# Three Winograd quads instead of two in the gate/up blocks of a macaron layer, with silu in one ScalarE pass and the carry moved to GpSimd DMAs

## The chip, the core and the metric

The kernel runs on one core of a Trainium2 chip. The metric is the device time of one execution in microseconds, the median of several runs. The core has five engines with an instruction stream each: TensorE (PE in the profile; its weight loads are PEld), VectorE (DVE), ScalarE (ACT), GpSimd (POOL) and SyncE (SP). Data comes from HBM into SBUF by DMA; TensorE accumulates into PSUM banks. SP issues the weight loads; GpSimd issues some other DMAs.

## The reference

One layer on 256 tokens of width 2048, in float32: a feed-forward network (FFN 1), a mixer with an RWKV-7 branch and a pooling branch, and a second feed-forward network (FFN 2). Each part is normed before and after and added to the residual. Only the feed-forward networks are touched by the change:

```python
def _swiglu(x, w_gate, w_up, w_down):
    return (jax.nn.silu(x @ w_gate) * (x @ w_up)) @ w_down
...
f = _swiglu(_rmsnorm(h, ln_ffn1_pre[l]), ffn1_gate[l], ffn1_up[l], ffn1_down[l])
h = h + MACARON_WEIGHT * _rmsnorm(f, ln_ffn1_post[l])
```

Gate and up are 2048 x 5632, down is 5632 x 2048. All of it is in float32.

## The kernel before

**Products in three matmuls.** Each float32 operand is split into a high part (rounded to the matmul's float32r format) and a low part (the rest). ScalarE makes the high part of a weight tile (`wH`, a cast), VectorE the low part (`wL`, a subtraction). `mm3` (lines 171 to 175) forms one product as high x high, high x low and low x high: three matmuls of 128 x 128 by 128 x 512.

**Blocks of gate and up.** `ffn` (line 611) runs over 11 blocks of 512 hidden columns. A block multiplies 16 row groups (k) of 128 with the gate columns and then with the up columns, for two halves of 128 tokens: 16 x 2 x 2 = 64 products. Blocks 0 and 1 do all 64 (`gemm_tok`, `gemm_at`). Blocks 2 to 10 (`FAST`, line 49) go through `seven` (line 315).

**Quads.** `seven` takes two weight row groups, the first two quads' worth from the front of k, and treats them as a 2 x 2 by 2 x 2 block product (rows k and k+1, the two token halves, and the two column groups, here gate and up). In Winograd's form this needs seven products instead of eight, at the price of sums: of the activations (`sums`, line 252, made once per FFN in block 1 and kept) and of the weights, in each block. `quad` (line 351) loads two weight tiles `a` and `b` by four DMAs, forms `t13` and `t24` on VectorE (lines 367, 372, 373), and splits `a`, `b`, `t13` and `t24` into high and low parts (lines 379, 380). Its products go to four extra PSUM banks (`p1`, `p5`, `p6`, `p7`) and to the four ordinary ones (`f0`, `f1`, `l0`, `l1`). The remaining rows go in pairs (`pair`, line 342): one load of two row groups, one cast, one subtraction, four products. `spots` says after which pair of gate (part 0) and of up (part 1) a quad stands. After the last quad `merge` (line 396) copies one bank and adds the others on VectorE (line 404), calls `ev_first` for the gate's half, and at the block's end `finish` (line 412) adds the up half and calls `ev_last`.

**Evictions.** In the fast blocks `ev_f` (line 635) lets ScalarE write a sigmoid into a free PSUM bank and VectorE multiply (line 638); `ev_l` (line 641) multiplies gate and up and turns the result by VectorE's 32 x 32 block transposes (`turn`, line 566) into the tile `T1`. In blocks 0 and 1 `ev_g` and `ev_gm` do sigmoid and multiplication, and `ev_um` the rest.

**The carry.** The block transposes leave the 32 x 32 blocks in the wrong places. `carry_at` (line 584) moves them in the next block, by 16 ScalarE copies of 32 partitions x 256 (line 594) into the tile `x32`, then makes the high part (one cast, line 598) and the low part (one subtraction, line 602) of the next four row groups of `hT`, the input of down.

**Down.** `post` (line 719) runs down over four groups of 512 columns, two at a time, each pair through `seven` with 44 row groups: 6 quads in the first pair of columns and 8 in the second (`NQ`, `QUADS`, lines 47 and 48). Their activation sums are made at the start of down.

**Order of the work.** The streams of TensorE, ScalarE and VectorE are written out by a planner: `put` appends a piece of TensorE work with its duration (`MM` = 0.2265 us a matmul) to a clock, `at` puts another piece of work at a planned time, and `run` (line 110) emits all in order of these times. Each engine then runs its stream strictly in that order. `slot` (line 104) gives a split the planned time at which the buffer used `WS_BUFS` = 5 splits earlier is free:

```python
    def slot(s, end):
        s.uses.append(end)
        n = len(s.uses) - 1 - WS_BUFS
        return s.uses[n] if n >= 0 else n - 1.0
```

SP's and GpSimd's streams are ordered by the scheduler. Raw weights land in `W32_BUFS` = 4 buffers of 512 KB; all other large tiles share 33 units of 512 KB (`NUNITS`).

Of the kernel before, what the change touches and what calls it, by code (L numbers as in the profile page):

```python
# [46 lines left out]
NQ = {False: 6, True: 8}  # L47
QUADS = {False: ((8, 12), (0, 3, 6, 9)), True: ((2, 4, 6, 8, 10, 12), (1, 3))}
FAST = range(2, 11)

# [5 lines left out]
class Block:  # L56
# [195 lines left out]
    def sums(s, T, out, when, own=None):  # L252
# [6 lines left out]
        def first():  # L259
            xH, xL = T[len(out) // 2]  # L260
            x = tt["x"] = s.unit((P, 2, 2, S), F32, "sx")
            V.tensor_tensor(out=fl(x), in0=xH.bitcast(F32).rearrange("p k t -> p (k t)"),
                            in1=xL.bitcast(F32).rearrange("p k t -> p (k t)"), op=ALU.add)

        def second():
            x = tt["x"]
            a11, a21 = x[:, :, 0, :P], x[:, :, 0, P:]
            a12, a22 = x[:, :, 1, :P], x[:, :, 1, P:]
            f = tt["f"] = s.unit((P, 4, 2, P), F32, "sf")
            V.scalar_tensor_tensor(out=f[:, 0], in0=a21, scalar=-1.0, in1=a22, op0=ALU.mult,  # L270
                                   op1=ALU.subtract)
            V.scalar_tensor_tensor(out=f[:, 1], in0=f[:, 0], scalar=-1.0, in1=a11,
                                   op0=ALU.mult, op1=ALU.subtract)
            V.tensor_tensor(out=f[:, 2], in0=a11, in1=a21, op=ALU.subtract)
            V.tensor_tensor(out=f[:, 3], in0=a12, in1=f[:, 1], op=ALU.subtract)
# [26 lines left out]
        def third():  # L302
            tt["H"], tt["L"] = [s.unit((P, 4, 2, P), F32R, n_) for n_ in ("sH", "sL")]
            nc.scalar.copy(fl(tt["H"]), fl(tt["f"]))

        def fourth():
            f, fH, fL = tt["f"], tt["H"], tt["L"]
            V.tensor_tensor(out=fl(fL), in0=fl(f), in1=fl(fH).bitcast(F32), op=ALU.subtract)
            for i in range(2):
                out.append([(fH[:, m, i], fL[:, m, i]) for m in range(4)])  # L310
# [4 lines left out]
    def seven(s, wf, cf, wl, cl, at, KT, T, sm, n, spots, ev_first, ev_last, trail=False):  # L315
# [35 lines left out]
        def quad(q):  # L351
# [18 lines left out]
            def t24():  # L370
                o = v["t24"]
                V.tensor_tensor(out=o[:, 0], in0=v["a"][:, 0], in1=v["t13"][:, 1], op=ALU.add)
                V.tensor_tensor(out=o[:, 1], in0=v["b"][:, 0], in1=o[:, 0], op=ALU.subtract)
# [8 lines left out]
            for t, fn in ((a, get), (a, t13), (a, t24), (a, lambda: split("a", 2)),  # L382
                          (b, lambda: split("b", 1)), (c, lambda: split("t13", 2)),
                          (d, lambda: split("t24", 2))):
                s.at(t, fn)
# [10 lines left out]
        def merge():  # L396
# [9 lines left out]
            for j, a in enumerate(((1, "p6", 0), (2, "p7", 1), (3, "p5", 2), (1, "p5", 1),  # L406
                                   (1, "f0", 1), (3, "f1", 3))):
                s.at(m + 0.7 + 0.1 * j, lambda a=a: add(*a))
            s.at(m + 4, lambda: ev_first(0, u[1], bank["p1"]))
            s.at(m + 4.6, lambda: ev_first(1, u[3], bank["p6"]))  # L410

        def finish(h):
            o = u[2 * h]
            V.tensor_tensor(out=o, in0=bank[f"l{h}"], in1=o, op=ALU.add)
            ev_last(h, o)
# [10 lines left out]
        if trail:  # L426
            s.by_half(wl, cl, stop, KT, s.clk, AHEAD[0],
                      lambda k, h: mul(f"l{h}", rows(k, h), ws[k]), keep, finish)
            return
# [136 lines left out]
    def turn(s, T1, h, src):  # L566

        s.nc.vector.transpose(out=T1[:, h * 512:h * 512 + 512], in_=src)  # L568

    def shuffle_split(s, T1, T, j):  # L570

        nc = s.nc
        x32 = s.unit((P, 4, S), F32, "x32")
        src = T1.rearrange("p (h k j c) -> p h k j c", h=2, k=4, j=4)
        dst = x32.rearrange("p k (h i c) -> p h k i c", h=2, i=4)
        for i in range(4):
            for q in range(4):
                nc.scalar.copy(dst[q * 32:q * 32 + 32, :, :, i],
                               src[i * 32:i * 32 + 32, :, :, q])
        dH, dL = T[j]  # L580
        nc.scalar.copy(dH, x32)
        nc.vector.tensor_tensor(out=dL, in0=x32, in1=dH.bitcast(F32), op=ALU.subtract)

    def carry_at(s, T1, T, t):
# [4 lines left out]
        def one(i, q):  # L589
            src = T1[0].rearrange("p (h k j c) -> p h k j c", h=2, k=4, j=4)  # L590
            if not x:
                x.append(s.unit((P, 4, S), F32, "x32"))
            dst = x[0].rearrange("p k (h i c) -> p h k i c", h=2, i=4)
            nc.scalar.copy(dst[q * 32:q * 32 + 32, :, :, i], src[i * 32:i * 32 + 32, :, :, q])  # L594

        def high():
            T.extend(s.new_T(1))
            nc.scalar.copy(T[-1][0], x[0])

        def low():  # L600
            dH, dL = T[-1]
            nc.vector.tensor_tensor(out=dL, in0=x[0], in1=dH.bitcast(F32), op=ALU.subtract)
        for n in range(16):
            s.at(t + 0.9 * n, lambda n=n: one(n // 4, n % 4))
        s.at(t + 15, high)
        s.at(t + 17, low)
# [4 lines left out]
    def ffn(s, wg, wu, wd, uT, rs, gpost, resid, emit, reload, xs=None):  # L611
# [7 lines left out]
        def block(b):  # L619
# [8 lines left out]
            def ev_g(h, ps):  # L628
                sg = s.tmp("sg")
                nc.scalar.activation(out=sg, in_=ps, func=AF.Sigmoid, scale=rs[h])  # L630
                nc.vector.scalar_tensor_tensor(out=sg, in0=ps, scalar=rs[h], in1=sg,
                                               op0=ALU.mult, op1=ALU.mult)
                sig[h] = sg

            def ev_f(h, u, free):
                nc.scalar.activation(out=free, in_=u, func=AF.Sigmoid)
                sig[h] = u
                s.at(s.now + 1.2, lambda: nc.vector.tensor_tensor(
                    out=u, in0=u, in1=free, op=ALU.mult))

            def ev_l(h, o):
                nc.vector.tensor_tensor(out=o, in0=o, in1=sig[h], op=ALU.mult)
                turned(h, o)

            def ev_gm(h, ps):
                sg = s.tmp("sg")
                nc.scalar.activation(out=sg, in_=ps, func=AF.Sigmoid, scale=r[h])
                sig[h] = sg
                s.at(s.now + 1.2, lambda: nc.vector.scalar_tensor_tensor(
                    out=sg, in0=ps, scalar=r[h], in1=sg, op0=ALU.mult, op1=ALU.mult))  # L650
# [18 lines left out]
            if b == 1:  # L669
                st["nT"], st["su"] = s.normed(uT, st["rb"], s.clk + 4), []  # L670
                s.sums(st["nT"], st["su"], s.clk + 16)
            nT, su = st["nT"], st["su"]
            if b in FAST:
                s.seven(wg, b * 512, wu, b * 512, s.T_at(nT), NKD, nT, su, 2, ((4,), (1,)),
                        ev_f, ev_l)
                return
            x = at if b == 1 else s.T_at(nT)
            s.gemm_at(wg, b * 512, x, NKD, ev_gm)
# [40 lines left out]
    def post(s, wd, at, KT, gpost, fac, resid, emit, reload, hT=None, sm=None):  # L719
# [52 lines left out]
        if hT is not None:  # L772
# [3 lines left out]
            for c in (0, 2):  # L776
                ev = ev_of(c)
                s.seven(wd, c * 512, wd, c * 512 + 512, at, KT, hT, sm, NQ[c == 2], QUADS[c == 2],
                        lambda h, u, _, ev=ev: ev(h, u), ev_of(c + 1), c == 2)
# [761 lines left out]
```

## Time and profile before

| | |
|---|---|
| time, median of 3 runs (lowest, highest) | 2059.87 us (2057.18, 2060.95) |
| the profiled execution's own time | 2060.43 us |
| its span, first to last instruction | 2058.7 us |
| granted TensorE clock, mean | 0.999 |
| TensorE / VectorE / ScalarE / GpSimd busy | 2043.5 / 1687.5 / 1247.4 / 76.0 us |
| DMA traffic | 407.03 MB, mean 198 GB/s |

The profile is of one execution. A group row gives the line, engine, operation, output and inputs with their shapes and the count, then busy time and mean duration of one, then the idle time of the engine just before them and what ended it. A timeline row gives start, duration, engine, line and operation, with "xN" where N in a row are merged. A window row gives, for a stretch of the span, the busy time and instruction count of each engine, the granted clock, the DMA engines' share and their rate.

### The profile page before, as it was taken

Reading aid. Unit: us, or ns where it says so; the run is one execution under the profiler, and the core shown is the slowest. Engines: PE = TensorE matmul, PEld = TensorE weight load, DVE = VectorE, ACT = ScalarE, POOL = GpSimd, SP = SyncE. Lnnn points to the kernel's source line nnn. Section 1 sums busy time; section 2 is a strip of 40 time slices with the busy share of each in tenths; the row PEclk is TensorE's granted clock in tenths of the full one; section 3 lists DMA queues with packets and bytes.
Section 4 is the critical chain, followed back from the end, with each engine's and each line's share of the span. In section 5 each row is a group of like instructions: output and inputs, shape, how many; then the busy total and the mean of one; then the engine's idle time right before and its main releaser. Section 6 shows DMA issues by size and latency. Waiting matters only on the chain.

```text
span 2058.7 us, 29579 instructions
## 1 busy us (share of the span) xinstructions
PE 2043.5 (99%) x10901; PEld 1721.7 (84%) x10901; DVE 1687.5 (82%) x2188; ACT 1247.4 (61%) x1788; POOL 76.0 (4%) x161
## 2 busy tenths in 40 slices
PE   9999999999999999999999999999999999999998
PEld 7888888888888899999888888888888888888886
DVE  6898889888988865799688667578988898889886
ACT  7667666776555574474465444466677666765553
POOL 0000000000000000000110110010000000000000
PEclk9999999999999999999999999999999999999999
DMA  7566666665667766656456565665666666656674
GB/s 259 175 195 211 194 206 194 196 212 176 210 208 251 228 189 187 180 159 196 133 155 193 161 245 189 205 211 169 203 199 200 214 195 194 197 186 215 210 254 155
DMA packets 226170, 407.03 MB, mean 198 GB/s; under 512 B 15199, under 2 KB 51177, under 8 KB 226025
## 3 DMA queue, kind: packets, MB, share of 16 engines
q1 hardware_dynamic: 219849, 384.69, 59.7%
q0 software_dynamic: 5888, 19.93, 2.7%
q8 instruction: 85, 1.39, 0.3%
q10 hardware_dynamic: 288, 0.52, 0.1%
q14 instruction: 60, 0.49, 0.1%
HBM read 396.69 MB, written 8.39 MB: 197 GB/s over the span
## 4 chain that ended last, share of the span: by engine, by line
PE 92%; DVE 3%; issue 2%; DMA 2%; ACT 1%; POOL 0%; POOLq 0%; DVEq 0%; SPq 0%; ACTq 0%
PE mm L173 24%; PE mm L175 23%; PE mm L174 23%; PE mc L523 10%; PE ms L175 3%; PE ms L173 3%; PE ms L174 3%; DMA w<-in_ffn_down_dram 1%; DVE wL L150 1%; PE tr L551 1%; ACT x L594 0%; PE pA L1262 0%; ACT wH L149 0%; DVE u L404 0%; ACT wH L379 0%
## 5 line engine op out<-in xcount | busy, mean ns | idle before, releaser
L150 DVE TENSOR_TENSOR wL<-w,wH 128x1024 fp32r<-128x1024 f32 (+2 forms) x597 | 711.4, 1206 | 232.9 <-ACT wH L149 229.9
L149 ACT CAST wH<-w 128x1024 fp32r<-128x1024 f32 (+2 forms) x597 | 614.8, 1043 | 392.4 <-PE mm L175 200.5
L173 PE MATMUL mm<-wH,xH 128*128 128x512 f32 x2076 | 811.6, 392 | 0.0
L175 PE MATMUL mm<-wH,xL 128*128 128x512 f32 x2076 | 808.5, 389 | 0.7 <-DVE xL L559 0.5
L174 PE MATMUL mm<-wL,xH 128*128 128x512 f32 x2076 | 808.4, 389 | 0.7 <-DVE wL L150 0.7
L175 PEld LDWEIGHTS mm<-wH,xL 128*128 128x128 f32 x2076 | 389.7, 188 | 82.8 <-DVE xL L559 1.5
L174 PEld LDWEIGHTS mm<-wL,xH 128*128 128x128 f32 x2076 | 389.8, 188 | 81.2 <-DVE wL L150 1.6
L173 PEld LDWEIGHTS mm<-wH,xH 128*128 128x128 f32 x2076 | 389.6, 188 | 81.0 <-ACT xH L557 0.2
L379 ACT CAST wH<-t 128x1024 fp32r<-128x1024 f32 x128 | 134.5, 1052 | 72.7 <-DVE t L367 42.6
L380 DVE TENSOR_TENSOR wL<-t,wH 128x1024 fp32r<-128x1024 f32 x128 | 152.5, 1218 | 25.0 <-ACT wH L379 25.0
L379 ACT CAST wH<-w 128x1024 fp32r<-128x1024 f32 (+1 forms) x128 | 107.2, 838 | 96.7 <-PE mm L175 51.6
L523 PE MATMUL mc<-xH,wH 128*128 128x256 f32 x560 | 159.5, 285 | 0.0
L523 PE MATMUL mc<-xL,wH 128*128 128x256 f32 x560 | 158.4, 283 | 0.0
L523 PE MATMUL mc<-xH,wL 128*128 128x256 f32 x560 | 158.4, 283 | 0.0
L594 ACT COPY x<-T 32x256 f32<-32x256 f32 x352 | 142.2, 404 | 10.9 <-DVE T L568 4.6
L380 DVE TENSOR_TENSOR wL<-w,wH 128x1024 fp32r<-128x1024 f32 (+1 forms) x128 | 116.7, 950 | 1.3 <-ACT wH L379 1.3
L523 PEld LDWEIGHTS mc<-xH,wH 128*128 128x128 f32 x560 | 106.0, 189 | 1.1
L523 PEld LDWEIGHTS mc<-xH,wL 128*128 128x128 f32 x560 | 106.0, 189 | 0.2
L523 PEld LDWEIGHTS mc<-xL,wH 128*128 128x128 f32 x560 | 106.0, 189 | 0.1
L367 DVE TENSOR_TENSOR t<-w,w 128x1024 f32<-128x1024 f32 x64 | 78.0, 1218 | 16.4 <-DMA w<-in_ffn_down_dram 12.0
L174 PE MATMUL ms<-wL,sH 128*128 128x512 f32 x164 | 63.8, 389 | 0.0
L175 PE MATMUL ms<-wH,sL 128*128 128x512 f32 x164 | 63.8, 389 | 0.0
(298 smaller groups left out, 1974.7 us busy)
## 6 DMA issues: line engine op xcount, KB each, us to landing
w<-in_ffn_up_dram SPq DMA_DIRECT2D x140, 512.0 KB
w<-in_ffn_gate_dram SPq DMA_DIRECT2D x138, 512.0 KB
w<-in_w_in_dram SPq DMA_DIRECT2D x128, 512.0 KB
w<-in_ffn_down_dram SPq DMA_DIRECT2D x120, 512.0 KB
w<-in_ffn_down_dram SPq DMA_DIRECT2D x112, 256.0 KB
w<-in_ffn_gate_dram SPq DMA_DIRECT2D x76, 256.0 KB
w<-in_ffn_up_dram SPq DMA_DIRECT2D x72, 256.0 KB
w<-in_w_out_dram SPq DMA_DIRECT2D x32, 512.0 KB
```

The lines of the kernel that those rows point to most:

```text
L149: s.nc.scalar.copy(vH, v)
L150: s.nc.vector.tensor_tensor(out=vL, in0=v, in1=vH.bitcast(F32), op=ALU.subtract)
L173: nc.tensor.matmul(ps, aH, bH, start=start, stop=False)
L174: nc.tensor.matmul(ps, aH, bL, start=False, stop=False)
L175: nc.tensor.matmul(ps, aL, bH, start=False, stop=stop)
L367: V.tensor_tensor(out=v["t13"], in0=v["a"], in1=v["b0"].to_broadcast([P, 2, 512]), op=ALU.subtract)
L379: nc.scalar.copy(H, v[n_])
L380: V.tensor_tensor(out=L, in0=v[n_], in1=H.bitcast(F32), op=ALU.subtract)
L523: s.nc.tensor.matmul(o, lh, rh, start=one and n == 0, stop=k == KT - 1 and n == 2, skip_group_check=True)
L551: nc.tensor.transpose(ps[:, i], src[:, i * P:(i + 1) * P], s.ident)
L594: nc.scalar.copy(dst[q * 32:q * 32 + 32, :, :, i], src[i * 32:i * 32 + 32, :, :, q])
```

## The change

- Blocks 2 to 10 do three quads instead of two (`NG`, `SPOTS`: after the third and fifth pair of gate and the second of up), so five pairs remain in gate and in up. The third quad's activation sums are made in block 1, by a `sums` of one quad (`nq=1`).
- The first column pair of down does seven quads instead of six.
- Silu is one ScalarE pass in place of a sigmoid and a VectorE multiplication, in all blocks; in the fast blocks it is done in place.
- The carry's 16 ScalarE copies become 16 DMAs issued by GpSimd, each of 32 partitions x 1 KB. For that `turn` writes `T1` in another order (four runs of 1 KB a partition). The high and low parts are made by halves, 10, 12, 13 and 15 us after the DMAs' planned time.
- VectorE's order: in a quad `t24` is formed in two steps that stand between the splits; two additions of the merge change places; at the end of a fast block both additions come first, then both multiplications, then both transposes.

The diff, cut to its core (`shuffle_split`, which nothing calls, also goes):

```diff
-NQ = {False: 6, True: 8}
-QUADS = {False: ((8, 12), (0, 3, 6, 9)), True: ((2, 4, 6, 8, 10, 12), (1, 3))}
+NQ = {False: 7, True: 8}
+QUADS = {False: ((8, 12), (0, 3, 5, 7, 9)), True: ((2, 4, 6, 8, 10, 12), (1, 3))}
+CARRY = (10, 13)
+NG, SPOTS = 3, ((2, 4), (1,))
...
-            def t24():
-                o = v["t24"]
-                V.tensor_tensor(out=o[:, 0], in0=v["a"][:, 0], in1=v["t13"][:, 1], op=ALU.add)
-                V.tensor_tensor(out=o[:, 1], in0=v["b"][:, 0], in1=o[:, 0], op=ALU.subtract)
+            def t2():
+                V.tensor_tensor(out=v["t24"][:, 0], in0=v["a"][:, 0], in1=v["t13"][:, 1],
+                                op=ALU.add)
+
+            def t4():
+                V.tensor_tensor(out=v["t24"][:, 1], in0=v["b"][:, 0], in1=v["t24"][:, 0],
+                                op=ALU.subtract)
...
-            for t, fn in ((a, get), (a, t13), (a, t24), (a, lambda: split("a", 2)),
-                          (b, lambda: split("b", 1)), (c, lambda: split("t13", 2)),
+            for t, fn in ((a, get), (a, t13), (a, lambda: split("a", 2)), (a, t2),
+                          (b, lambda: split("b", 1)), (b, t4), (c, lambda: split("t13", 2)),
                           (d, lambda: split("t24", 2))):
...
-            for j, a in enumerate(((1, "p6", 0), (2, "p7", 1), (3, "p5", 2), (1, "p5", 1),
+            for j, a in enumerate(((1, "p6", 0), (2, "p7", 1), (1, "p5", 1), (3, "p5", 2),
                                    (1, "f0", 1), (3, "f1", 3))):
...
+        def total(h):
+            V.tensor_tensor(out=u[2 * h], in0=bank[f"l{h}"], in1=u[2 * h], op=ALU.add)
...
+        def both():
+            total(0)
+            total(1)
+            ev_last((u[0], u[2]))
...
-        s.nc.vector.transpose(out=T1[:, h * 512:h * 512 + 512], in_=src)
+        dst = T1.rearrange("p (j h k c) -> p h k j c", j=4, h=2, k=4)[:, h]
+        s.nc.vector.transpose(out=dst, in_=src.rearrange("p (k j c) -> p k j c", k=4, j=4))
...
-            nc.scalar.copy(dst[q * 32:q * 32 + 32, :, :, i], src[i * 32:i * 32 + 32, :, :, q])
+        def move():
+            x.append(s.unit((P, 4, 2, 4, 32), F32, "x32"))
+            src = T1[0].rearrange("p (j h k c) -> p j h k c", j=4, h=2, k=4)
+            for i in range(4):
+                for q in range(4):
+                    nc.gpsimd.dma_start(out=x[0][q * 32:q * 32 + 32, i],
+                                        in_=src[i * 32:i * 32 + 32, q])
...
-        for n in range(16):
-            s.at(t + 0.9 * n, lambda n=n: one(n // 4, n % 4))
-        s.at(t + 15, high)
-        s.at(t + 17, low)
+        s.at(t, move)
+        for h in range(2):
+            s.at(t + CARRY[h], lambda h=h: high(h))
+            s.at(t + CARRY[h] + 2, lambda h=h: low(h))
...
             def ev_g(h, ps):
-                sg = s.tmp("sg")
-                nc.scalar.activation(out=sg, in_=ps, func=AF.Sigmoid, scale=rs[h])
-                nc.vector.scalar_tensor_tensor(out=sg, in0=ps, scalar=rs[h], in1=sg,
-                                               op0=ALU.mult, op1=ALU.mult)
-                sig[h] = sg
+                sig[h] = s.tmp("sg")
+                nc.scalar.activation(out=sig[h], in_=ps, func=AF.Silu, scale=r[h])
...
-            def ev_f(h, u, free):
-                nc.scalar.activation(out=free, in_=u, func=AF.Sigmoid)
+            def ev_f(h, u):
                 sig[h] = u
-                s.at(s.now + 1.2, lambda: nc.vector.tensor_tensor(
-                    out=u, in0=u, in1=free, op=ALU.mult))
...
-            def ev_l(h, o):
-                nc.vector.tensor_tensor(out=o, in0=o, in1=sig[h], op=ALU.mult)
-                turned(h, o)
+                nc.scalar.activation(out=u, in_=u, func=AF.Silu)
+
+            def ev_l(o):
+                for h in range(2):
+                    nc.vector.tensor_tensor(out=o[h], in0=o[h], in1=sig[h], op=ALU.mult)
+                for h in range(2):
+                    turned(h, o[h])
...
                 s.sums(st["nT"], st["su"], s.clk + 16)
+                s.sums(st["nT"], st["su"], s.clk + 27, nq=1)
...
-                s.seven(wg, b * 512, wu, b * 512, s.T_at(nT), NKD, nT, su, 2, ((4,), (1,)),
-                        ev_f, ev_l)
+                s.seven(wg, b * 512, wu, b * 512, s.T_at(nT), NKD, nT, su, NG, SPOTS,
+                        ev_f, ev_l, one_end=True)
```

## What I predicted, before the run

> **What bounds the kernel now.** I read the page's head first, then the busy times of single stretches, then TensorE's own timeline.
>
> ```profile
> span 2058.7 us, 29579 instructions
> ...
> PE 2043.5 (99%) x10901; PEld 1721.7 (84%) x10901; DVE 1687.5 (82%) x2188; ACT 1247.4 (61%) x1788; POOL 76.0 (4%) x161
> ```
>
> ```profile
> core 0: us, PE busy (x) PEld busy (x) DVE busy (x) ACT busy (x) POOL busy (x), PEclk, DMA share, GB/s
> 227.40:269.60 42.20, 42.20 (x188) 34.95 (x187) 37.43 (x42) 28.96 (x40) 0.00 (x0) 1.00 0.63 200
> 480.40:522.50 42.10, 41.06 (x180) 33.33 (x179) 37.26 (x48) 27.20 (x41) 0.00 (x0) 1.00 0.56 170
> ```
>
> ```profile
> 224.61 0.39 PE L173 MATMUL mm<-wH,xH 128*128 128x512 f32 x1
> ...
> 268.13 0.39 PE L173 MATMUL mm<-wH,xH 128*128 128x512 f32 x1
> ```
>
> TensorE is busy all the time, also in the first stretch, which is one gate/up block with two quads: no gap in 42.20 us at full clock (PEclk 1.00). The second stretch, the end of FFN 1's gate/up, has the one larger hole outside the tail, 42.10 - 41.06 = 1.04 us. The two matmul rows are 192 matmuls apart, so one matmul takes 43.52/192 = 0.2267 us, and one product of `mm3` (three matmuls) 0.680 us. A block has 16 x 4 - 2 = 62 products, 62 x 0.680 = 42.2 us, which is the stretch. So the time is the number of products, as long as the other engines keep ahead; VectorE, 37.43 of 42.20 us, is the one close behind.
>
> **TensorE's part.** A quad does two weight rows of two output columns in seven products instead of eight. The change adds one quad in each of blocks 2 to 10 (9 blocks, 2 FFNs) and one in the first column pair of each down: 18 + 2 = 20 products less, 20 x 0.680 = **13.6 us**. No other step leaves or joins TensorE. The profiled execution took 2060.43 us (span 2058.7), 0.56 above the median of the three runs, 2059.87; so the sum is 2060.43 - 13.60 = 2046.83 in its terms and 2046.3 against the median, if nothing new makes TensorE wait.
>
> **VectorE's part.** The rows of the same block:
>
> ```profile
> 227.48 0.68 DVE L414 TENSOR_TENSOR u<-mm,u 128x512 f32<-128x512 f32 x1
> 228.19 0.69 DVE L642 TENSOR_TENSOR u<-u,u 128x512 f32<-128x512 f32 x1
> 228.92 0.71 DVE L568 STREAM_TRANSPOSE T<-u 128x512 f32<-128x512 f32 x1
> 229.55 0.65 DVE L414 TENSOR_TENSOR u<-mm,u 128x512 f32<-128x512 f32 x1
> ...
> 231.60 1.18 DVE L150 TENSOR_TENSOR wL<-w,wH 128x1024 fp32r<-128x1024 f32 x1
> 232.71 1.22 DVE L367 TENSOR_TENSOR t<-w,w 128x1024 f32<-128x1024 f32 x1
> 233.96 0.69 DVE L372 TENSOR_TENSOR t<-w,t 128x512 f32<-128x512 f32 x1
> 234.68 0.69 DVE L373 TENSOR_TENSOR t<-w,t 128x512 f32<-128x512 f32 x1
> 235.29 1.82 DVE L380 TENSOR_TENSOR wL<-w,wH 128x1024 fp32r<-128x1024 f32 x2
> 237.03 2.35 DVE L380 TENSOR_TENSOR wL<-t,wH 128x1024 fp32r<-128x1024 f32 x2
> ...
> 260.49 2.73 DVE L404 TENSOR_TENSOR u<-ms,u 128x512 f32<-128x512 f32 x4
> 263.26 1.29 DVE L404 TENSOR_TENSOR u<-mm,u 128x512 f32<-128x512 f32 x2
> 264.46 1.22 DVE L150 TENSOR_TENSOR wL<-w,wH 128x1024 fp32r<-128x1024 f32 x1
> ...
> 267.32 1.28 DVE L638 TENSOR_TENSOR u<-u,ms 128x512 f32<-128x512 f32 x2
> 268.52 1.22 DVE L150 TENSOR_TENSOR wL<-w,wH 128x1024 fp32r<-128x1024 f32 x1
> ```
>
> What counts is start to start. A 1024-wide operation costs 1.13 (the two at 237.03, 2.35 - 1.22); I take 1.14. A 512-wide one costs 0.72 when the next reads its result (227.48 to 228.19, 233.96 to 234.68) and 0.60 to 0.63 when it does not (228.92 to 229.55, 234.68 to 235.29); 1024-wide with a reader behind it, 1.25 (232.71 to 233.96). A quad today takes 232.71 to 237.03 and two more subtractions, 4.32 + 2.27 = 6.59; in the new order nothing reads what was written just before: 4 x 1.14 + 3 x 0.60 = 6.34. Per block: the new quad +6.34; one pair less in gate and one in up, -2.27; the two multiplications of silu, 268.52 - 267.32 = -1.20; the two old quads reordered, -0.50; the merge, now 3.97, with one dependent step instead of four or so, -0.26; the end, 231.60 - 227.48 = 4.12, as six operations at about 0.61, -0.47; the carry's subtraction in halves, +0.07. Together 37.43 + 1.71 = **39.1 us of 41.5**, 94% instead of 89%. The transpose writes 128-byte runs further apart; no row has that form, and I take its 0.71 unchanged (twice 0.71 would be +1.4 a block, in the rival below).
>
> The Trainium skill, "VectorE: DVE Perf Modes", section "The DRAIN you can't avoid", speaks against the reordering: the pipeline empties after every operation before the next starts, whatever the order. By that rule the 1.48 us of the three reorderings would not come and the block would hold 40.6. The rows (0.72 against 0.60) disagree, and I go by them.
>
> **Whether 94% is enough** is a question of order, not of sums. Count from TensorE's first product of a block: three pairs (2.72 each), quad 1 at 8.15 (4.76 long), two pairs, quad 2 at 18.35, two pairs of up, quad 3 at 28.54, three pairs to 41.5. A split may start when TensorE leaves the buffer used five splits earlier, plus about 0.2 (a matmul row is 0.39 long, 0.16 more than the spacing). Weights land in four buffers, each reloaded only after VectorE's subtraction has read it:
>
> ```profile
> 452.65 4.20 DMA w<-in_ffn_up_dram
> ...
> 511.25 4.91 DMA w<-in_ffn_down_dram
> ```
>
> ```profile
> 254.54 6.43 SPq L135 DMA_DIRECT2D w<-in_ffn_gate_dram  x5
> ```
>
> ```profile
> 258.26 1.05 ACT L149 CAST wH<-w 128x1024 fp32r<-128x1024 f32 x1 [1.80 <-DMA w<-in_ffn_gate_dram]
> ```
>
> A load thus takes 3.7 (issued 254.54 by SP, cast at 258.26) to 4.9 us; I take 4.2. The walk: the first up pair's subtraction starts at 19.7. From there VectorE hardly rests: l0, l1 to 22.1, a carry half, quad 3 and the other half to 29.7, l2 to 31.0, l3, l4 and the next block's first pair to 34.6. The next block's second pair is loaded into l2's buffer, 31.0 + 4.2 = 35.2, cast to 36.2, subtracted to 37.4; the merge stands behind it and frees the bank that TensorE opens the next block with at 40.6. **Slack there: 0.9 us** (today, with the merge at 260.49 and the block's end near 269.6, some 5). Then one subtraction (42.2), quad 1's first three operations (45.1) and the end (48.8), its other two small ones and the t13 split: done 9.6 into the next block, needed at 10.2; t24 at 10.8, needed 11.6. **Slack 0.6 and 0.8.** Quad 2 is ready 2 us early, and by l0 VectorE waits again, so no lateness adds up from block to block. The forecast is that TensorE stays nearly fed, with some 0.1 us lost in an average block: the additional packets of the carry and a load of 4.9 eat most of a 0.6 to 0.9 slack.
>
> **The carry.**
>
> ```profile
> L594 ACT COPY x<-T 32x256 f32<-32x256 f32 x352 | 142.2, 404 | 10.9 <-DVE T L568 4.6
> ```
>
> ```profile
> 703.72 2.53 POOL L1491 DMA_DIRECT2D hsp<-fg  x4 [1.08 <-DVE fg L768]
> ...
> 971.33 1.98 POOL L1346 DMA_DIRECT2D w<-in_rwkv_g_dram  x4
> ```
>
> ```profile
> DMA to landing us min/median/max: 2.5/2.7/4.1
> ```
>
> Sixteen ScalarE copies a block (352 in all, 0.404 each, 6.5 us a block) leave. ScalarE has 28.96 of 42.20 us; with a new quad's four casts for two pairs' two (+1.7 by the 1.05 of the cast above, one of them half as wide) it falls to about 24, and nothing gets faster by that in the steady blocks. In their place stand 16 GpSimd DMAs of 32 partitions. The nearest rows are the four L1346 ones, also of 32 partitions: 0.495 each, landing after 2.7 us (4.1 at most). GpSimd has nothing else in this stage (0.00 above), so its queue holds nobody up. T1 is complete at 7.3 in the walk; 16 x 0.495 = 7.9; the last lands at 17.9. The new wait is ScalarE's first half copy, planned at 18.0, and behind it in order stand the casts of l0, l1 and quad 3. So it just fits, and since l0 may be 0.9 late before a bank is missed, the decision falls at about 18.9. The carry's 0.5 MB a block adds little to the 0.63 DMA share.
>
> The Trainium skill, "DMA: Bandwidth & Descriptors", section "Rules for kernel authors", says to coalesce: under 64 KB a transfer is mostly overhead; these are 32 KB. Here the four issued in 1.98 us, each landing in 2.7, overlap, so that only the last one's overhead stays; the rule would decide only if they ran singly.
>
> **Costed at nothing.** The third sum of block 1 adds some 2.3 us of VectorE in the block where two gate multiplications (1.4) leave. Silu needs its table:
>
> ```profile
> L630 ACT ACT_TABLE_LOAD x1 | 1.3, 1283 | 0.0
> ```
>
> One load stands before FFN 1's first sigmoid (x1), and none inside the blocks, though casts and sigmoids alternate there. I expect the same of silu, and one to three loads more where the mixer's sigmoids follow, 1.3 us of ScalarE each, behind TensorE's work; a swap around every silu would be 2.6 us a block and fall under the first rival. Down's seventh quad meets the same ratio with more room (two pairs to a quad, about 8.6 of 10.2 us). In the 1.04 us hole at the end of FFN 1, ScalarE's carry copies stand between its casts; up to 1 us may come back.
>
> **Rivals.**
> A, VectorE and the four buffers become the bound: loads of 4.9 us or more and a dearer transpose use up both slacks, and 0.25 to 0.8 us is lost in each of 18 blocks, 4.5 to 14 us: 2051 to 2061, middle 2056. For it: 94%, slacks under 1 us. Against: 2.4 us of rest per block are left and lateness heals.
> B, the other side: the carry lands late. If a DMA costs GpSimd 0.63 as the four of L1491 do (2.53/4), 10.1 replaces 7.9, and the last lands at 20.1, or 21.5 with 4.1 us; that is 1.2 to 2.6 past 18.9, times 18 blocks 22 to 47 us, less 13.6: 2068 to 2093, around 2070. It costs more than the quads give from a landing at 18.9 + 0.75 = 19.7 on. For it: ScalarE waits in order. Against: L1491's rows have 128 partitions, the carry's 32. (Singly, 16 x 2.7 = 43 us a block, they would more than halve the speed of the stage; the four in 1.98 us exclude it.)
> C, the change does not do what it says: reordering brings nothing, quad 1 in the next block is 0.7 later and its slack gone, some 0.5 us a block, 9 us: 2055. The 0.72 and 0.60 of the rows speak against it. This is the time that the rule of the Trainium skill, "VectorE: DVE Perf Modes", would give.
>
> **How the numbers follow.** Forecast: 2046.3 and 0.1 x 18 = about 2, **2048** (with the hole of FFN 1 regained 2045.3 at best), chance 0.58. A 0.22, half of it faster by over 0.2%, half within. B 0.16, slower. C 0.04, at the edge, counted within. Under 0.2% (4.1 us) a measurement cannot tell from no change. So faster 0.69, same 0.15, slower 0.16. The range goes from 2045 to A's far end and a little over, 2063, and leaves B out.
>
> **What would show it.** Right: a gate/up block of about 41.5 us with TensorE gapless, VectorE near 39 in it, and the sixteen DMAs ended before ScalarE's half copy asks. Step by step: dependent pairs gone from VectorE's rows; no table load inside a block; merge ending less than 1 us before the next block. Wrong: TensorE idle behind L404 adds or L380 splits (A), ScalarE idle before the carry's cast on a DMA (B).

## The result and the profile after

The changed kernel takes 2066.44 us (median of 7 runs, 2064.80 to 2069.17), the kernel before 2059.87 (7 runs, 2057.18 to 2060.95): ratio 1.0034, 95% interval [1.0023, 1.0046]. It is slower by 6.6 us, where 2048.0 was forecast; the range, 2045 to 2063, missed it too. The profiled execution took 2066.3 us.

From the page after, the span, the busy times and two groups of instructions:

```profile
span 2064.6 us, 30104 instructions
...
PE 2037.2 (99%) x10841; PEld 1709.5 (83%) x10841; DVE 1725.6 (84%) x2278; ACT 1131.1 (55%) x1502; POOL 248.9 (12%) x513
...
L175 PE MATMUL mm<-wH,xH 128*128 128x512 f32 x1956 | 766.9, 393 | 10.5 <-DVE u L414 7.5
...
L601 POOL DMA_DIRECT2D x<-T x352 | 172.8, 499 | 754.5 <-issue 484.9
```

The 60 matmuls, 20 products, have gone (10901 to 10841) and with them 13.6 us. The span grew by 5.9 all the same, so about 19.5 us of newly lost time stand in TensorE's way (12.2 of them show as idle time of PE, 27.4 us against 15.2; the rest the profile counts as busy, some 1.6 of it matmuls at half clock). Single blocks of the changed kernel, by the busy times of stretches (length, then busy time and count of PE, PEld, DVE, ACT, POOL, then clock, DMA share, GB/s):

```profile
223.80:265.90 42.10, 41.78 (x183) 34.20 (x183) 39.30 (x46) 23.46 (x27) 7.83 (x16) 1.00 0.68 215
265.90:308.70 42.80, 42.15 (x183) 34.04 (x183) 39.31 (x46) 23.48 (x27) 7.84 (x16) 1.00 0.66 209
392.40:439.40 47.00, 42.71 (x185) 34.05 (x183) 39.32 (x46) 23.26 (x27) 7.86 (x16) 1.00 0.61 191
```

A block of 61 products should be 61 x 0.680 = 41.5 us. These are 42.1, 42.8 and 47.0, at full clock. The loss is uneven: the block of 47.0 and one of 45.5 (from the first `ms` product at 1745.26 to the next block's at 1790.74) hold 9.5 of the 19.5 us. VectorE does 39.3 in each, ScalarE 23.5, GpSimd 7.84: the sums are those of the prediction (39.1, about 24, 7.9). So what fails is when the work comes, not how much there is. VectorE's rows of the changed kernel show the reordering at work:

```profile
280.00 1.22 DVE L374 TENSOR_TENSOR t<-w,w 128x1024 f32<-128x1024 f32 x1
...
284.08 2.51 DVE L390 TENSOR_TENSOR wL<-t,wH 128x1024 fp32r<-128x1024 f32 x2
...
305.48 2.73 DVE L414 TENSOR_TENSOR u<-ms,u 128x512 f32<-128x512 f32 x4
308.13 1.28 DVE L414 TENSOR_TENSOR u<-mm,u 128x512 f32<-128x512 f32 x2
309.33 1.21 DVE L152 TENSOR_TENSOR wL<-w,wH 128x1024 fp32r<-128x1024 f32 x1
...
313.33 1.28 DVE L423 TENSOR_TENSOR u<-mm,u 128x512 f32<-128x512 f32 x2
...
315.73 1.29 DVE L589 STREAM_TRANSPOSE T<-u 128x512 f32<-128x512 f32 x2
316.95 0.65 DVE L390 TENSOR_TENSOR wL<-w,wH 128x512 fp32r<-128x512 f32 x1
```

A quad is 284.08 - 280.00 and two subtractions of 1.14, 6.36 us (forecast 6.34; its own terms, 4 x 1.14 + 3 x 0.60, make 6.36); the merge 309.33 - 305.48 = 3.85 (3.71); the block's end 316.95 - 313.33 = 3.62 (3.65). Both transposes with 128-byte runs cost 1.22 start to start, no more than before.

What is new is a wait of ScalarE. From the views of waits, of GpSimd's DMA line (all 352 DMAs, then the first nine and the other seven of the row at 274.75) and of GpSimd's and ScalarE's timelines of the changed kernel:

```profile
ACT xH L613 <- DMA x<-T: 30.1, 20, 4.5
...
PE mm L175 <- DVE u L414: 7.5, 9, 1.9
```

```profile
DMA to landing us min/median/max: 1.6/3.4/6.3
...
DMA to landing us min/median/max: 1.7/2.5/3.2
...
DMA to landing us min/median/max: 4.7/5.2/5.9
```

```profile
274.75 7.84 POOL L601 DMA_DIRECT2D x<-T  x16 [34.28 <-issue]
...
404.23 5.39 POOL L601 DMA_DIRECT2D x<-T  x11 [36.99 <-ACT wH L151]
409.96 0.99 POOL L601 DMA_DIRECT2D x<-T  x2 [0.33 <-DMA x<-T]
411.77 1.48 POOL L601 DMA_DIRECT2D x<-T  x3 [0.82 <-DMA x<-T]
```

```profile
284.27 1.06 ACT L389 CAST wH<-t 128x1024 fp32r<-128x1024 f32 x1 [1.89 <-DVE t L382]
286.90 0.62 ACT L613 CAST xH<-x 128x512 fp32r<-128x512 f32 x1 [1.57 <-DMA x<-T]
287.43 1.99 ACT L151 CAST wH<-w 128x1024 fp32r<-128x1024 f32 x2
```

In 20 blocks ScalarE stands still before the carry's half copy (L613), 30.1 us in all. In the block that opens at 265.9 the DMAs start at 274.75 and all sixteen are issued by 282.59 (274.75 + 7.84); the last has landed when the cast starts, at 286.9, that is 4.3 us later and 21.0 after the block's start. Landings are counted from a DMA's issue; they grow along the row, so the median of all, 3.4, is too low for the DMA that ends the wait. Behind it in order stand the casts of the first two up pairs, l0 and l1 (287.43). At the block's end the same lateness shows once more as the wait of the next block's first matmul for the merge (L414). In the block at 392.4 it is worse: GpSimd starts at 404.23 only, 3.5 us after the transposes ended (elsewhere mostly 0.5; the view puts the wait down to a cast of ScalarE, and why GpSimd needs it stays open), and waits twice for an earlier one of its own DMAs; ScalarE then idles 4.5 us.

### The profile page after: what moved, and what is told of

The parts are those of the page before. It is cut to its first block, busy times and chain, and to the rows that moved or that the text cites. A ratio compares the mean times of both kernels' runs of the same rounds, so it can differ in the third digit from the quotient of the medians.

```text
span 2064.6 us, 30104 instructions
## 1 busy us (share of the span) xinstructions
PE 2037.2 (99%) x10841; PEld 1709.5 (83%) x10841; DVE 1725.6 (84%) x2278; ACT 1131.1 (55%) x1502; POOL 248.9 (12%) x513
## 5 line engine op out<-in xcount | busy, mean ns | idle before, releaser
L152 DVE TENSOR_TENSOR wL<-w,wH 128x1024 fp32r<-128x1024 f32 (+2 forms) x557 | 661.0, 1206 | 233.3 <-ACT wH L151 228.4
L175 PE MATMUL mm<-wH,xH 128*128 128x512 f32 x1956 | 766.9, 393 | 10.5 <-DVE u L414 7.5
L151 ACT CAST wH<-w 128x1024 fp32r<-128x1024 f32 (+2 forms) x557 | 569.9, 1041 | 357.9 <-PE mm L177 171.8
L176 PE MATMUL mm<-wL,xH 128*128 128x512 f32 x1956 | 763.0, 390 | 2.2 <-DVE wL L152 2.2
L177 PE MATMUL mm<-wH,xL 128*128 128x512 f32 x1956 | 762.8, 390 | 0.7 <-DVE xL L579 0.7
L175 PEld LDWEIGHTS mm<-wH,xH 128*128 128x128 f32 x1956 | 367.5, 188 | 93.0 <-issue 12.7
L389 ACT CAST wH<-t 128x1024 fp32r<-128x1024 f32 x168 | 177.0, 1053 | 280.5 <-DVE t L382 198.1
L601 POOL DMA_DIRECT2D x<-T x352 | 172.8, 499 | 754.5 <-issue 484.9
L390 DVE TENSOR_TENSOR wL<-t,wH 128x1024 fp32r<-128x1024 f32 x168 | 203.2, 1220 | 9.2 <-ACT wH L389 5.9
L390 DVE TENSOR_TENSOR wL<-w,wH 128x1024 fp32r<-128x1024 f32 (+1 forms) x168 | 159.2, 948 | 1.3 <-ACT wH L389 1.3
L175 PE MATMUL ms<-wH,sH 128*128 128x512 f32 x168 | 65.5, 390 | 0.0
```

The costliest lines, as they stand in the source:

```text
L151: s.nc.scalar.copy(vH, v)
L152: s.nc.vector.tensor_tensor(out=vL, in0=v, in1=vH.bitcast(F32), op=ALU.subtract)
L175: nc.tensor.matmul(ps, aH, bH, start=start, stop=False)
L176: nc.tensor.matmul(ps, aH, bL, start=False, stop=False)
L177: nc.tensor.matmul(ps, aL, bH, start=False, stop=stop)
L389: nc.scalar.copy(H, v[n_])
```

## The experiments

Theory 1: **the late carry** alone costs the 19 us (Rival B's mechanism). Theory 2: **the bank at the block's start** does, VectorE being too full for the merge to come in time (Rival A's). All ratios are against the kernel before on the same chip.

**e1: the half copies 4 us later.**

```diff
-CARRY = (10, 13)
+CARRY = (14, 17)
```

> The changed kernel with one constant other: ScalarE's half copies of the carry planned 4 us later (14 and 17 us after the DMAs' planned time instead of 10 and 13). Nothing else moves. Theory 1 (the carry lands late: ScalarE, in order, waits 1.5 us a block for the GpSimd DMAs, the casts of up's first pairs stand behind it, VectorE idles and frees the bank for the next block late): that wait goes, and with it nearly all of TensorE's 19 us of holes; 2047 to 2051. Theory 2 (the load of gate's second pair, 1.4 us late in front of the merge in VectorE's order): the holes at the block starts stay, only those inside a block go; 2057 to 2062. Theory 3 (VectorE simply full at 94 per cent): 2060 to 2066.

Measured: 2046.55 us (2045.43 to 2047.46), ratio 0.9936 [0.9921, 0.9951]. From its page, one block of it, and the end of the transposes and the DMAs in that block:

```profile
PE 2031.7 (99%) x10841; PEld 1712.2 (84%) x10841; DVE 1730.3 (85%) x2278; ACT 1137.0 (56%) x1502; POOL 248.1 (12%) x513
```

```profile
263.75:305.18 41.43, 41.43 (x185) 34.31 (x184) 39.59 (x47) 23.88 (x27) 7.81 (x16) 1.00 0.68 216
```

```profile
271.36 1.29 DVE L589 STREAM_TRANSPOSE T<-u 128x512 f32<-128x512 f32 x2
...
273.19 7.81 POOL L601 DMA_DIRECT2D x<-T  x16 [33.59 <-issue]
```

No wait of the half copy on a DMA is left, and no hole of TensorE in a gate/up block, though a DMA takes no less time to land (1.6/3.4/5.9 us). The carry as a whole is done sooner all the same: counted from the block's first product, at 265.65, T1 is complete at 7.0, the DMAs begin at 7.5, and the last lands at 19.3 (issued at 280.5, landing 4.5 later). So some of the change's lateness is its own effect, handed on from block to block. One constant is worth 19.9 us. The block is 41.43 us with VectorE busy for 39.59 of it: 96% is enough, and the forecast's figure is reached.

**e4: the merge ahead of the next block's second gate pair,** the carry as late as in the change.

```diff
-            s.at(m + 0.2, start)
+            s.at(m - 0.3, start)
...
-                s.at(m + 0.7 + 0.1 * j, lambda a=a: add(*a))
+                s.at(m - 0.2 + 0.01 * j, lambda a=a: add(*a))
```

> The changed kernel with the merge's copy and six additions planned 0.5 to 1.4 us earlier, so that in VectorE's and ScalarE's order they stand ahead of the next block's second gate pair and not behind its load. The carry stays as it is. Theory 2 (load in front of the merge): the holes at the block starts, about 11 of 19 us, go: 2053 to 2057. Theory 1 (late carry): the block starts gain what the merge is moved ahead, but the same lateness hits the next splits and the holes inside the blocks (7 us) stay: 2056 to 2062. Theory 3 (VectorE full): the wait moves to the next quad's splits; 2062 to 2066.

Measured: 2050.66 (2049.84 to 2052.39), ratio 0.9957 [0.9942, 0.9972], below every range that I gave. The waits view of this kernel:

```profile
ACT xH L613 <- DMA x<-T: 27.4, 19, 4.7
```

ScalarE still waits 27.4 us for the carry, and yet 15.8 of the 19.9 us are gone, with the holes at the block starts. Both theories hold a part: the carry makes the lateness, the bank that opens the next block is where most of it is paid. With the bank freed earlier, 1.4 us of waiting in each of 19 blocks are for the most part made good.

**e5: both together.**

```diff
-CARRY = (10, 13)
+CARRY = (14, 17)
...
-            s.at(m + 0.2, start)
+            s.at(m - 0.3, start)
```

> The late half copies (14 and 17 us) and the merge ahead of the next block's second gate pair, together. Theory 1 (the late carry alone stops the gate/up blocks; with late half copies no gap was left in them, 2046.55): nothing is left for the merge to mend, 2045.5 to 2047.5. Theory 2 (the merge at the block start is a bound of its own): 2 us or more below 2046.5.

Measured: 2047.08 (2046.51 to 2047.33), ratio 0.9940 [0.9925, 0.9955], as with the late half copies alone. Without the lateness the bank is no bound.

**e7: the carry as four DMAs of 128 partitions,** half copies where the change has them. The 32 x 32 blocks stay in the wrong places.

```diff
-            for i in range(4):
-                for q in range(4):
-                    nc.gpsimd.dma_start(out=x[0][q * 32:q * 32 + 32, i],
-                                        in_=src[i * 32:i * 32 + 32, q])
+            for i in range(4):
+                nc.gpsimd.dma_start(out=x[0][:, i], in_=src[:, i])
```

> The change with its half copies where it has them (10 and 13 us), but the carry as four DMAs of 128 partitions x 1 KB in place of sixteen of 32 partitions. The bytes are the same, the 32 x 32 blocks stay where the transposes left them. Theory 1a (the carry is late because sixteen issues of 0.49 us stand in a row and the last one has its landing after that): T1 is there at 8.3 us after the block's start, four issues take 2 to 2.5 us, the last lands some 5 us later, at 16, ahead of the cast planned at 18.0: no wait of ScalarE on it, 2046 to 2048.5. Theory 1b (what takes long is moving 0.5 MB from SBUF to SBUF beside the weight loads, in however many pieces): still late by 2 us in most blocks, 2058 to 2066.

Measured: 2045.91 (2045.57 to 2046.28), ratio 0.9935 [0.9920, 0.9950]. From its timelines of GpSimd and ScalarE, and its DMA line:

```profile
272.27 2.16 POOL L600 DMA_DIRECT2D x<-T  x4 [39.06 <-issue]
```

```profile
282.73 0.61 ACT L611 CAST xH<-x 128x512 fp32r<-128x512 f32 x1
```

```profile
DMA to landing us min/median/max: 1.9/3.8/5.4
```

The same 512 KB, issued in 2.16 us instead of 7.84, have landed long before the cast asks, and the gain is all there, although one DMA takes no less time to land. It is sixteen issues in a row that make the carry late, not the bytes. The Trainium skill, "DMA: Bandwidth & Descriptors", section "Rules for kernel authors", which says to coalesce transfers under 64 KB, agrees in direction. What decided here was the issue time, 16 x 0.49 us, of which 5.7 us went; the landing of the last one gave another 1 us (3.2 after its issue ended, at 277.65).

**e9, e11, e12: where the half copies stand.** Only the constant differs.

```diff
-CARRY = (10, 13)
+CARRY = (12, 15)
...
+CARRY = (11, 14)
...
+CARRY = (8, 11)
```

> The half copies at 12 and 15 us after the DMAs' planned time, between the change's 10 and 13 and the later 14 and 17; nothing else differs from the change. The first cast then stands at 20.0 us after the block's start, behind l0's cast, while the last DMA lands near 20.9 (in a few blocks near 23). Late-carry theory: ScalarE waits 0.5 to 1 us in most blocks and 2 to 3 us in the few with a late start of GpSimd; most of that is taken up by the slack of 0.6 to 0.9 us, so 2047 to 2052, nearer to the later setting than to the change. If instead the place in ScalarE's order matters only by whether l0 and l1 are both ahead of it: no nearer than half way, 2054 to 2060.

> Half copies at 11 and 14 us after the DMAs' planned time, nothing else differs from the change (10 and 13). With 12 and 15 the first half copy stands behind the casts of the first two up pairs, and the time is 2047.1; with 10 and 13 it stands ahead of both, 2066.4. Theory of place (what costs is which casts stand behind the waiting copy): with the copy between the two, or still ahead of both but 1 us later in the plan, the time falls stepwise: 2047 to 2050 if the first cast stands ahead of it, 2062 to 2067 if none does. Theory of lateness (each us by which the copy is planned nearer to the landing brings the same): half way, 2054 to 2059.

> Half copies at 8 and 11 us after the DMAs' planned time, nothing else differs from the change (10 and 13). The DMAs land when they did; the first copy now stands at 16.0 after the block's start, ahead of casts of the second quad too, and ScalarE waits in front of them until 20 or 21. Theory of place: quad 2's products, needed from 18.4 on, come 2 to 3 us late in each of 20 blocks or so, on top of the change: 2090 to 2130. Theory that the waiting costs little where loads and buffers are ahead: below 2075.

| CARRY | median (lowest, highest), us | ratio [95% interval] |
|---|---|---|
| 8, 11 | 2069.95 (2067.83, 2072.00) | 1.0054 [1.0040, 1.0068] |
| 10, 13 (the change) | 2066.44 (2064.80, 2069.17) | 1.0034 [1.0023, 1.0046] |
| 11, 14 | 2052.56 (2051.64, 2053.36) | 0.9968 [0.9955, 0.9981] |
| 12, 15 | 2047.12 (2046.28, 2048.27) | 0.9944 [0.9930, 0.9957] |
| 14, 17 | 2046.55 (2045.43, 2047.46) | 0.9936 [0.9921, 0.9951] |

ScalarE's timeline in the same block, first with (12, 15), then with (8, 11):

```profile
283.89 1.05 ACT L151 CAST wH<-w 128x1024 fp32r<-128x1024 f32 x1 [0.48 <-PE mm L177]
285.25 1.05 ACT L151 CAST wH<-w 128x1024 fp32r<-128x1024 f32 x1 [0.31 <-PE mm L177]
286.21 0.61 ACT L613 CAST xH<-x 128x512 fp32r<-128x512 f32 x1
```

```profile
284.43 1.06 ACT L389 CAST wH<-t 128x1024 fp32r<-128x1024 f32 x1 [1.89 <-DVE t L382]
286.82 0.62 ACT L613 CAST xH<-x 128x512 fp32r<-128x512 f32 x1 [1.33 <-DMA x<-T]
287.35 1.05 ACT L151 CAST wH<-w 128x1024 fp32r<-128x1024 f32 x1
288.30 0.61 ACT L613 CAST xH<-x 128x512 fp32r<-128x512 f32 x1
288.82 1.05 ACT L151 CAST wH<-w 128x1024 fp32r<-128x1024 f32 x1
```

The time goes in steps, not with the plan's microseconds: from 10 to 11 it falls by 13.9, from 12 to 14 by 0.6. With (12, 15) the casts of l0 and l1 stand ahead of the half copy; it waits for a DMA in two blocks alone, those with the latest carries (4.1 us in all), and TensorE has one hole of 1.2 us behind them. With (11, 14) l0's stands ahead, l1's behind; five waits of 13.3 us in all are left, in the blocks where the carry lands latest, and with them some 5.5 us of time. That lies between what place alone and lateness alone gave. My own figure for (8, 11), 2090 and more, was wrong: in the order that came out the copy still stands behind quad 2's last cast (284.43), so the same casts wait as in the change, and only the second half copy has moved, ahead of l1's.

**e6: VectorE's order taken back,** late half copies kept: in the quad, in two additions of the merge, and at the block's end.

```diff
-            for t, fn in ((a, get), (a, t13), (a, lambda: split("a", 2)), (a, t2),
-                          (b, lambda: split("b", 1)), (b, t4), (c, lambda: split("t13", 2)),
+            for t, fn in ((a, get), (a, t13), (a, t2), (a, t4), (a, lambda: split("a", 2)),
+                          (b, lambda: split("b", 1)), (c, lambda: split("t13", 2)),
...
-            total(0)
-            total(1)
-            ev_last((u[0], u[2]))
+            for h in range(2):
+                total(h)
+                ev_last(h, u[2 * h])
```

> Late half copies, and VectorE's order taken back in the quad (both t24 steps ahead of the splits), in the merge's additions and at the fast block's end (add, multiply, transpose by halves); three quads and silu in one pass stay. If the order is worth the 1.2 to 1.5 us a block of VectorE that the rows of before gave and the slacks of the prediction (0.9, 0.6, 0.8 us) are as narrow as it worked them out: VectorE some 40.7 us a block, 0.3 to 0.6 us lost in each of 18 blocks, 2052 to 2057, with holes behind L414 or the t13 split. If the order brings VectorE time but the slack is wider: VectorE higher by some 25 us over the whole span and 2046 to 2048. If the order brings nothing at all (every operation drains first): VectorE's sum unchanged within 5 us, 2046.5.

Measured: 2057.03 (2055.02 to 2060.50), ratio 0.9988 [0.9979, 0.9997]: 10.5 us above the new order, at the upper end of the first theory's range. Two of TensorE's waits and a quad of VectorE in this kernel:

```profile
277.16 0.50 PE L176 MATMUL ms<-wL,sH 128*128 128x512 f32 x1 [0.17 <-DVE wL L390]
...
435.35 0.47 PE L175 MATMUL mm<-wH,xH 128*128 128x512 f32 x1 [0.61 <-DVE u L414]
```

```profile
280.43 1.22 DVE L374 TENSOR_TENSOR t<-w,w 128x1024 f32<-128x1024 f32 x1
...
284.75 2.35 DVE L390 TENSOR_TENSOR wL<-t,wH 128x1024 fp32r<-128x1024 f32 x2
```

The old quad is 284.75 - 280.43 and 2 x 1.14, 6.60 us, 0.24 longer; with the merge (3.97) and the end (4.13) the block gets 1.3 to 1.4 us of VectorE more. TensorE then waits at the places that the walk named, at quad 1's t13 split (277.16, a product into an `ms` bank) and at the bank that opens a block (435.35).

If every operation had to drain first, the order would have brought nothing and this kernel would have stood at 2046.5. The Trainium skill, "VectorE: DVE Perf Modes", section "The DRAIN you can't avoid", says so of an operation in general, and adds in the same paragraph that a next operation that is not held starts earlier; the prediction took up the first half alone. The trace agrees with the second half: in the block's end, where no operation reads the one before it, six of some 0.69 us follow each other by 0.60 (313.33 to 316.95 in the change).

**e8: sigmoid and a VectorE multiplication in the fast blocks,** late half copies kept.

```diff
-            def ev_f(h, u):
-                sig[h] = u
-                nc.scalar.activation(out=u, in_=u, func=AF.Silu)
+            def ev_f(h, u, free):
+                nc.scalar.activation(out=free, in_=u, func=AF.Sigmoid)
+                sig[h] = u
+                s.at(s.now + 1.2, lambda: nc.vector.tensor_tensor(
+                    out=u, in0=u, in1=free, op=ALU.mult))
```

> Late half copies, and in the fast blocks silu as before: a sigmoid of ScalarE into a free bank and a VectorE multiplication 1.2 us later; the rest of the change stays. VectorE gets 1.2 us a block more, 40.5 of 41.5 us. If the prediction's walk is right, the t13 split of the next block's first quad (slack 0.6 us) comes 0.5 to 0.6 us late: 0.3 to 0.6 us in each of 18 blocks, 2052 to 2057. If VectorE has more room than the walk gave it: 2046 to 2048.

Measured: 2058.18 (2057.09 to 2061.17), ratio 0.9994 [0.9984, 1.0003]: 11.6 us above e1 for 1.2 us of VectorE a block, and 1 us above the range given. TensorE's waits are at the same two places:

```profile
321.49 0.50 PE L176 MATMUL ms<-wL,sH 128*128 128x512 f32 x1 [0.49 <-DVE wL L390]
...
438.10 0.47 PE L175 MATMUL mm<-wH,xH 128*128 128x512 f32 x1 [1.01 <-DVE u L414]
```

**e3: two quads, the rest of the change kept.**

```diff
-NG, SPOTS = 3, ((2, 4), (1,))
+NG, SPOTS = 2, ((4,), (1,))
...
-                s.sums(st["nT"], st["su"], s.clk + 27, nq=1)
```

> The changed kernel with two quads in the gate/up blocks again, at the old places, and without the third activation sum. Silu in one pass, the carry by DMA, VectorE's order and down's seventh quad stay. All theories: VectorE falls to about 35 of 42.2 us a block and takes up the carry's lateness, so TensorE runs without holes and only down's two products less show: 2057 to 2060. If the carry's wait alone stops TensorE even so: 2062 or more.

Measured: 2056.83 (2055.65 to 2057.57), ratio 0.9987 [0.9977, 0.9996]. The half copy waits for a DMA twice, 4.0 us in all, and no block has a hole: without the third quad the same carry is early enough. The copy also starts later there, behind casts that wait for TensorE (in one block it starts 13.8 us after T1 is complete; in the change, in the block shown, ScalarE is ready for it after 11.1), so e3 does not tell VectorE's rest from the order. With the third quad and late half copies it is 10.3 us less, for 18 products of 12.2.

**e2: the sixteen ScalarE copies back in place of the DMAs,** with the old order of `T1`; three quads and the rest stay.

```diff
-                    nc.gpsimd.dma_start(out=x[0][q * 32:q * 32 + 32, i],
-                                        in_=src[i * 32:i * 32 + 32, q])
...
+            nc.scalar.copy(dst[q * 32:q * 32 + 32, :, :, i], src[i * 32:i * 32 + 32, :, :, q])
...
+        for n in range(16):
+            s.at(t + 0.9 * n, lambda n=n: one(n // 4, n % 4))
```

> The changed kernel with the old carry: the transposes write as before and ScalarE makes the 16 copies, no GpSimd DMAs. Three quads, one-pass silu and VectorE's new order stay. Theory 1 (late carry): ScalarE waits for no DMA any more; 2047 to 2052, the copies costing ScalarE 6.5 us a block that it has. Theory 2 (load in front of the merge): 2056 to 2062. Theory 3 (VectorE full): 2060 to 2066.

Measured: 2084.53 (2083.43 to 2085.59), ratio 1.0120 [1.0105, 1.0135], far above what I expected. One stretch of a block, by busy times:

```profile
281.80:301.10 19.30, 19.29 (x86) 15.52 (x85) 16.72 (x17) 18.79 (x29) 0.00 (x0) 1.00 0.60 188
```

ScalarE has 29 instructions and 18.79 of 19.30 us there: the copies fall among the casts of quads 2 and 3, and the casts come late. Over the whole block it is busy for 30 of 43.5 us. TensorE's waits for the merge's bank grow to 16.3 us (7.5 in the change). The carry has to leave ScalarE's stream if there are to be three quads.

**e10: six quads in down's first column pair,** late half copies kept.

```diff
-NQ = {False: 7, True: 8}
+NQ = {False: 6, True: 8}
```

> Late half copies (14 and 17), and six quads again in the first column pair of down. Two products more in all, 2 x 0.680 = 1.4 us: 2047.9 if down had room for the seventh quad; 2046.5 or less if the seventh quad cost VectorE as much as it gave TensorE.

Measured: 2047.13 (2046.08 to 2050.23), ratio 0.9944 [0.9931, 0.9956], in another series of runs than e1 (0.9936 [0.9921, 0.9951]). The intervals overlap: whether the seventh quad brings its 1.4 us stays open; it costs no more than it brings.

## Why the prediction was wrong, point by point

**The step that failed is the carry's landing.** The prediction had T1 complete at 7.3 us, 7.9 of issuing, a landing of 2.7 for the last one: 17.9, against a cast planned at 18.0. Measured in the block at 265.9, T1 was complete at 8.3 (the merge ends past the block's start, not before it), GpSimd began at 8.85, the issuing took 7.84, and the last one landed 4.3 after that: 21.0, or 3.1 us later than forecast. The first error is less than that. In e1, where no cast waits, the last one lands at 19.3, 1.4 us later than forecast: 0.5 between T1 and the first issue, which the sum had at nothing, and 1.3 in the landing, less 0.4 for an earlier T1 and a shorter issuing. That is past the point of decision, 18.9. Counted the same way, from the block's first product, the change has 20.7; the further 1.4 us are the lateness coming back: late casts make a late merge, a late T1 and so a later carry in the next block. "No lateness adds up from block to block" failed with it.

The 2.7 was the median of two rows of four DMAs, loads of 64 KB from HBM. The sixteen, 32 KB from SBUF to SBUF, have 3.4, and up to 6.3, and in the row shown the last seven have 4.7 to 5.9. The DMA engines' share differs little (0.60 in the stretch of the first four, 0.61 to 0.68 here). Why the landing grows from the tenth on was not tried.

**Rival B is what happened,** with a smaller price. Its point of decision (18.9) and its break-even (19.7) were passed by 21.0, so the sign came out as B had it. Its formula, 18 x (21.0 - 18.9) = 38 us, is twice the 19 to 20 measured; I take it that VectorE's and ScalarE's rest in the block makes half of the lateness good, but no run measures that share. B entered with 0.16, and it was left out of the range because L1491's rows have 128 partitions. Its way in was looked for in the issue cost, and that was right at 0.49; the landing, with a maximum of 4.1 us in the same row, was the weaker number.

**A fixed place was taken for a time.** The walk took the copy as planned at 18.0 and asked only whether the data are there. What counted was which casts stand behind it: moved 2 us, it stands behind l0's and l1's, and DMAs that take as long to land cost next to nothing (e9). That late copies are harmless follows too: nothing needs them before down.

**Right:** TensorE's 20 products (13.6 forecast; 12.7 in e1, 13.7 in e7; in e1 the hole at the end of FFN 1's gate/up is gone, and waits of 0.43 and 0.76 us stand in the last rows of FFN 1's down instead). VectorE's 39.1 of 41.5 us (39.59 of 41.43 in e1). The slacks of 0.9, 0.6 and 0.8 us: 1.2 to 1.4 us more of VectorE a block, in e6 and e8, cost 10.5 and 11.6 us, mostly at the very split and bank that the walk named, 0.58 and 0.65 us in each of 18 blocks. Rival C is refuted by e6. Rival A by itself is refuted by e1 and e5; its place, the bank, is where the lateness is paid (e4).

**What was costed at nothing.** The silu tables: this view of ScalarE's groups in the changed kernel

```profile
L650 ACT ACTIVATE u<-u 128x512 f32<-128x512 f32 x36 | 22.2, 633 | 41.3 <-DVE u L414 41.3
...
L896 ACT ACT_TABLE_LOAD x3 | 3.8, 1283 | 1.7 <-PE mm L177 1.6
...
L646 ACT ACT_TABLE_LOAD x2 | 2.6, 1283 | 0.0
```

has no load at the fast blocks' silu (L650), and two more loads in the whole kernel than before, within the one to three forecast. That nothing gets faster by the copies' leaving ScalarE was wrong for three quads: e2 is 38 us above e1.

## What to carry to other kernels

Where work moves from an engine's own stream to DMAs, its end is the pause before the first issue (0.5 us here), the issue time of all of them and the landing of the last, taken from the slow end of the measured landings; put the waiting instruction behind everything that does not need it, and count what stands behind it in order, not the microseconds of the wait. When an engine is 95% full, find the two or three instructions with the least slack: 1.2 us more a block, 22 us in 18 blocks, cost 11.6, while ScalarE's waits of 30 us cost 19.9 with the bank freed late and its 27 us cost 4.1 with the bank freed early (e4). The constant (14, 17) turns this change from 6.6 us slower to 13 us faster. Four DMAs bring as much time, but as e7 has them they do not move the blocks to their places.

## What the runs showed that was not expected

**TensorE at half clock after a short hole.** In the changed kernel, in one of its latest blocks, by the stretch and by TensorE's timeline:

```profile
1762.60:1766.20 3.60, 3.50 (x9) 2.77 (x10) 3.60 (x5) 2.29 (x4) 0.00 (x0) 0.53 0.63 193
```

```profile
1761.43 0.50 PE L175 MATMUL mm<-wH,xH 128*128 128x512 f32 x1 [1.00 <-ACT wH L151]
1762.69 0.71 PE L176 MATMUL mm<-wL,xH 128*128 128x512 f32 x1 [0.76 <-DVE wL L152]
1763.20 0.63 PE L177 MATMUL mm<-wH,xL 128*128 128x512 f32 x1
1763.63 0.63 PE L175 MATMUL mm<-wH,xH 128*128 128x512 f32 x1
```

After waits of 1.00 and 0.76 us with one matmul between them, the granted clock is 0.53 and matmuls follow each other by 0.43 us instead of 0.227, some eight of them, 1.6 us in all. The half rate lasts 3.4 us (0.50 from 1762.81 to 1766.22). Waits of 1.81 and 0.76 us in the same place of the block at 392.4 left the clock at 1.00, so the length of the hole alone does not decide. The Trainium skill, "TensorE: Matmul & The Clock Gate", section "Part 1: The HAM clock gate", has the half rate come after an idle window of about 3.4 us; here the waits were shorter, and no run shows such a window.

**GpSimd waits on its own DMAs.** In the rows at 404.23 to 411.77 above, the twelfth and the fourteenth issue waited until an earlier DMA of the same carry had landed, 0.33 and 0.82 us. By the trace's semaphores it is each time the DMA eight before: the program counts the DMAs on eight semaphores in turn, and these two issues came 0.28 us after the fourth and the sixth had landed (409.68 and 411.49). In 13 of 22 carries the sixteen go out without a pause.
